# A two-block network in float32 on one core: another order of the first loads

## The chip, the cores and the metric

The kernel runs on one core of one Trainium2 chip. The metric is the device time of one execution, in microseconds (us).

## The reference, cut to what matters

Two blocks run one behind the other on 256 tokens of 1024 features. The first has two layers; a context of 256 tokens goes through the first of them too, so that layer works on 512 columns. What the change touches is how a layer of the first block begins:

```python
mod = (silu_c @ w_mod[layer] + b_mod[layer])[:, None, :]
shift1, scale1, gate1, shift2, scale2, gate2 = jnp.split(mod, N_MOD, axis=-1)
h = modulate(rms_norm(x, norm_mix[layer]), shift1, scale1)   # h * (1 + scale) + shift
q, k, v, hy, g = jnp.split(h @ w_in[layer], PROJ_SPLITS, axis=-1)
...
h = jnp.sin(freq[0] * (z @ fw1 + fb1))                        # the hyena filter
h = jnp.sin(freq[1] * (h @ fw2 + fb2))
h = jnp.sin(freq[2] * (h @ fw3 + fb3))
h = (h @ fw4).reshape(length, 2, HYENA_WIDTH)
h = h * decay[:, None, :]
```

The filter does not depend on x. Its spectrum (a discrete Fourier transform) is wanted for the long convolution in the middle of the layer. Behind attention, convolution, gates and a feed-forward network of two layers comes a second block, which ends in a mixture of 32 experts whose weights alone are some 200 MB.

## The kernel before, in words

The data lie feature-major: 128 features on the partitions, tokens along the free axis. A weight tile (`u`, 128x1024 float32, 512 KB) holds 128 columns of a weight for all 1024 rows. Most products take float32 in two parts: ACT rounds a tile to its upper part (`u<-u`, fp32r), DVE subtracts it to get the lower part, and TensorE does three matmuls (upper by upper, upper by lower, lower by upper). Modulation tiles (`w_mod`) and the filter's are used as plain float32; such a matmul leaves two records in the trace.

Nothing is scheduled by hand. Generators (`modulation`, `statistics`, `spectra`, `hy_vx` and others) yield what their next step reads. `drive` steps the first of them whose inputs are there by a built-in estimate of each engine's time (`Timer`), and the engines then do their instructions in the order in which they were written. `Stream` loads weight tiles ahead of their use, `loads` of them, on SyncE's queue. All DMA issues of SyncE stand in one queue, and each new one also waits until the one eight issues of the queue before it has landed, since eight semaphores go round. All operations are written by one helper, line 288, so nearly every row of the trace reads L288 and instructions are known by their tiles.

At the start of `program`, SyncE issues the filter's three small inputs (`z`, `filt_w1`, `filt_w23`; `load_filter`), the column parameters (`cols`), the identity (`ident`) and x in four tiles (`load_x`). Then `layer` steps `spectra` once, which issues the filter's last weight w4 and its decay, and drives three generators together:

- `modulation(0, 0)`: 16 tiles of `w_mod`, two matmuls each (`ps<-u,cs`; two tiles use different column groups of TensorE), then a copy by ACT, four transposes, and DVE makes `mod` and `gmix`, the gain columns. `loads` is set by hand in it: eight modulation tiles ahead in the first half, a DFT table after the second step, three weight tiles from the fourth.
- `statistics`: ACT squares x (eight times `t<-u` or `acc<-u`, 128x512), DVE adds them up in `acc`, TensorE sums over the partitions with a column of ones, DVE and GpSimd take the reciprocal root, TensorE spreads it (`ps<-ident,s`), DVE multiplies x by it.
- `spectra`: three rounds of matmul (`ps<-t`, 128x256), reduction of the angle by DVE, and a sine by ACT (`t<-t`, 128x256); then the matmuls with w4 (`ps<-u,t`) and the two layers' spectra (`ps<-u`).

When the first two are through, `modulated` makes the layer's input: for each pair of chunks ACT scales half of it (`t<-t,mod,gmix`), DVE the other half, ACT takes the upper part (`u<-t`) and DVE the lower. `hy_vx` then starts the first projection with two weight units side by side (48 matmuls), and what is left of `spectra` runs beside it.

Of the kernel before, what the change touches and what calls it, by code (L numbers as in the profile page):

```python
# [19 lines left out]
KC = D // 128  # L20
# [13 lines left out]
# ---------------------------------------------------------------- host layout  # L34
# [6 lines left out]
def _units(w):  # L41
    """[K, N] -> [N/128, 128 rows, K/128, 128 columns]"""
    k, n = w.shape
    return np.ascontiguousarray(w.reshape(k // 128, 128, n // 128, 128).transpose(2, 1, 0, 3))


def column_parameters(p):
    """Every per-feature vector as columns of one [128, n] array, and where each one starts."""
# [32 lines left out]
def shape_tables():  # L81
    t = {}
    # axial rotary embedding of the first block, feature-major; the sign of the pair swap is in the sine
# [8 lines left out]
    # discrete Fourier transform on odd frequencies  # L92
# [7 lines left out]
    # filter positions and decay  # L100
# [10 lines left out]
    # rotary embedding of the second block: inverse frequency and sign of the swapped half, per partition  # L111
# [4 lines left out]
    # 8 * log of how many of the dilated branches let query i see key j  # L116
# [6 lines left out]
    # before[t', t] = t' < t; descending weights that break ties; slot numbers  # L123
# [45 lines left out]
# ---------------------------------------------------------------- order of the program  # L169

class Null:
    """Stands for every object of the program in the pass that only finds the order of the weight tiles."""
# [22 lines left out]
class Part:  # L195
    """The two float32r parts of a tile.  ready: the n pieces of the program that fill it are there; eta: when they
    are expected to have run."""
# [15 lines left out]
class Timer:  # L213
    """Estimates when each engine will be through with its instructions, and when each tile will be there."""
# [60 lines left out]
class Engine:  # L275
    """An engine whose instructions are also given to the timer."""
# [26 lines left out]
class Stream:  # L303
    """The weight tiles that one chain of generators uses, in their order.  Loads run ahead; a unit (128 columns) is
    split ahead into two float32r parts."""
# [20 lines left out]
    def prepare(self):  # L326
        """split the next unit"""
# [8 lines left out]
    def run(self):  # L336
        """loads and splits ahead"""
# [13 lines left out]
    def get(self, *key, unit=True):  # L351
        """the next tile: a generator, which ends with the tile, or with the two parts of a unit"""
# [23 lines left out]
class Squares:  # L376
    """Sums of the squares of x for each token.  x comes in four pairs of chunks, each [128, 2, T] cut as gemm cuts
    its output; the first three are added up before they are summed over the partitions"""
# [39 lines left out]
class Net:  # L418
# [28 lines left out]
    # ---- allocation  # L447
# [16 lines left out]
    def ahead_of(self, n):  # L464
        """split n weight units ahead"""
        self.W.loads, self.W.splits = n + self.MORE, n

    # ---- order of the instructions
    def defer(self, fn, *deps, engine="DVE"):
        """fn emits instructions of an engine once deps are expected to be there when the engine comes to them"""  # L470
        self.pending.append((deps, engine, fn))

    def tick(self):
        """deferred instructions whose inputs are there; loads and splits of weights"""
# [22 lines left out]
    def force(self):  # L497
        """the deferred instructions whose inputs are there first"""
        e = min(self.pending, key=self.when)
        self.pending.remove(e)  # L500
        e[2]()
# [9 lines left out]
    def stall(self, deps):  # L511
        """how long the tensor engine would wait"""
# [3 lines left out]
    def step(entry):  # L516
        """one step of [generator, what the step reads]; False if it can do nothing yet, None at its end"""
# [7 lines left out]
    def drive(self, *gens, extra=()):  # L525
        """all of the generators to their ends: the first of those whose inputs are there makes a step.  A generator
        yields what its next step reads, or BLOCK.  extra: entries that come second, but need not end"""
# [25 lines left out]
    def fill(self, *queues):  # L553
        """a step of the first entry of a queue, if its inputs are there"""
# [11 lines left out]
    def background(self):  # L566
        """a step of the work that only has to be done some time later"""
# [3 lines left out]
    def wait(self, *deps):  # L571
        """steps of the fillers while the tensor engine would wait"""
# [5 lines left out]
    def run(self, gen):  # L578
        """a generator to its end, with the fillers in its gaps"""
# [13 lines left out]
    # ---- pieces  # L593
    def divide(self, items, parts=(), then=None):
        """hi = float32r(src), lo = src - hi for each (hi, lo, src) or (hi, lo, src, factor of src); then the
        parts are ready"""
# [26 lines left out]
    def gemm(self, keys, xs, T=512, n=None, cuts=None, together=False, stream=None):  # L623
        """unit . xs for each weight unit, as a list of PSUM tiles [128 features, n units, T]; a generator.  xs may
        still grow to n; with cuts xs is a list of lists, and the k range between two cuts has its own output;
        together: the units side by side, each chunk of xs used as soon as it is there"""
# [50 lines left out]
    def pair(name, *idx, tail=()):  # L677
        """the two units of a pair of chunks: the last index counts pairs"""
# [3 lines left out]
    def by_tile(t, T):  # L682
        """[128, 2 chunks, T] cut as gemm cuts its output"""
# [5 lines left out]
    def pairs(self, T):  # L689
        """an endless row of tiles [128, 2, T]"""  # L690
# [5 lines left out]
    def chunks(self, n, T, pieces=1):  # L696
        """n places for the two float32r parts of [128, T]; and the parts of each two as gemm cuts its output"""
# [1663 lines left out]
```

## Time and profile before

| | |
|---|---|
| median of 3 runs | 2087.15 us (2084.54 to 2092.17) |
| span of the profiled execution | 2082.8 us; its own time is not listed apart |
| TensorE busy | 1986.3 us, 95% of the span |
| TensorE busy in the first 51 us | 36.57 us |
| DMA rate from 1700 to 1800 us | 419 GB/s |

A timeline row tells the start of a group of like instructions, the time from the group's start to its end, the engine, the operation with its tiles and sizes, how many there are, and, in brackets, how long the engine stood idle before it and what ended that. A window row tells busy times of the engines, the granted clock of TensorE (1.00 is full speed), the share of the DMA engines and their rate. A busy TensorE is not one at its peak, since ends of matmuls are modelled.

### The profile page before, as it was taken

What the parts mean: (1) busy time and instruction counts of PE and PEld (TensorE: products, weight loads), DVE (VectorE), ACT (ScalarE), POOL (GpSimd) and SP (SyncE); (2) the same over time, 40 slices, a digit from 0 to 9 for tenths busy, and PEclk for the clock granted to TensorE, in tenths of its full rate; (3) what the DMA queues carried; (4) which work ended last, traced back from release to release, by engine and by line L of the source; (5) the groups of instructions that cost most, each with busy time, mean ns of one, the idle gap of its engine ahead of it and who ended that gap; (6) DMA issues with size and microseconds to landing.
All of it is one profiled execution on the core that took longest, in us unless ns stands there. A gap on an engine that the chain in (4) does not pass through costs nothing. (4 is left out here: it accounts for less than half of the span.)

```text
span 2082.8 us, 28349 instructions
## 1 busy us (share of the span) xinstructions
PE 1986.3 (95%) x11415; PEld 1450.8 (70%) x11415; DVE 945.7 (45%) x1624; ACT 718.3 (34%) x1171; POOL 39.8 (2%) x49
## 2 busy tenths in 40 slices
PE   7999999999999999999999999999999898888886
PEld 3777877776778888889888999998799541111111
DVE  6665755145334333576764755568654310000001
ACT  3433665224222322363653543444734110000001
POOL 0000000000000000000000000000010000000000
PEclk9999999999999999999999999999999999999999
DMA  9423224464223233444357455553257999999997
GB/s 366 132 81 101 62 82 150 164 236 174 96 88 114 89 91 100 134 170 149 114 188 245 164 189 172 178 183 94 100 167 295 377 419 420 419 419 419 419 420 318
DMA packets 121438, 432.13 MB, mean 207 GB/s; under 512 B 13654, under 2 KB 14152, under 8 KB 121304
## 3 DMA queue, kind: packets, MB, share of 16 engines
q1 hardware_dynamic: 119464, 424.64, 55.7%
q0 software_dynamic: 1696, 5.38, 0.8%
q8 instruction: 91, 1.49, 0.3%
q14 instruction: 43, 0.35, 0.0%
q10 hardware_dynamic: 144, 0.26, 0.0%
HBM read 428.13 MB, written 2.10 MB: 207 GB/s over the span
## 5 line engine op out<-in xcount | busy, mean ns | idle before, releaser
L288 PE MATMUL ps<-u 128*128 128x256 f32 (+2 forms) x9088 | 1599.8, 345 | 28.1 <-DMA u<-w 15.9
L288 PEld LDWEIGHTS ps<-u 128*128 128x128 f32 (+1 forms) x9088 | 1289.0, 186 | 348.1 <-DMA u<-w 101.3
L288 DVE TENSOR_TENSOR u<-u 128x1024 fp32r<-128x1024 f32 (+4 forms) x414 | 433.1, 1071 | 269.6 <-ACT u L288 226.2
L288 ACT ACTIVATE u<-u 128x1024 fp32r<-128x1024 f32 (+3 forms) x392 | 360.3, 960 | 286.9 <-DVE u L288 237.0
L288 PE MATMUL ps<-u,t 128*32 128x512 f32 (+1 forms) x1028 | 214.9, 610 | 30.8 <-DMA u<-w 18.2
L288 PEld LDWEIGHTS ps<-u,t 128*32 128x32 f32 (+1 forms) x1028 | 44.2, 110 | 185.8 <-DMA u<-w 114.5
L288 ACT ACTIVATE u<-ps 128x512 f32<-128x512 f32 (+3 forms) x207 | 91.7, 488 | 237.0 <-PE ps L288 236.3
L288 DVE TENSOR_TENSOR t<-t,ps 128x512 f32<-128x512 f32 x12 | 8.3, 688 | 258.9 <-PE ps L288 258.9
L288 ACT ACTIVATE t<-ps 128x512 f32<-128x512 f32 x57 | 33.4, 595 | 252.5 <-PE ps L288 252.4
L288 DVE TENSOR_TENSOR u<-u,ps 128x512 f32<-128x512 f32 x53 | 36.4, 687 | 128.4 <-PE ps L288 128.3
L288 PE MATMUL ps<-u,cs 128*32 128x512 f32 x384 | 86.1, 644 | 0.0
L288 DVE TENSOR_TENSOR u<-ps,u 128x128 fp32r<-128x128 f32 (+2 forms) x135 | 59.6, 491 | 48.9 <-ACT u L288 42.7
L288 DVE SCALAR_TENSOR_TENSOR u<-ps,mod,u 128x256 f32<-128x256 f32 x96 | 41.7, 479 | 79.9 <-PE ps L288 79.6
L288 ACT ACTIVATE u<-t 128x512 fp32r<-128x512 f32 (+1 forms) x74 | 41.8, 592 | 102.9 <-DVE t L288 91.7
L288 ACT ACTIVATE u<-ps,s 128x512 fp32r<-128x512 f32 (+1 forms) x26 | 15.8, 640 | 149.0 <-PE ps L288 145.8
L288 DVE SCALAR_TENSOR_TENSOR u<-ps,s,u 128x512 fp32r<-128x512 f32 (+2 forms) x24 | 15.4, 662 | 113.2 <-ACT u L288 90.9
L288 ACT ACTIVATE t<-ps,s 128x256 f32<-128x256 f32 (+1 forms) x80 | 49.1, 620 | 41.2 <-DVE s L288 40.2
L288 POOL TENSOR_TENSOR s<-s,mhalf 128x4 f32<-128x4 f32 (+2 forms) x25 | 28.5, 1141 | 1608.4 <-DVE s L288 1527.1
L288 PE MATMUL ps<-ident,t 128*128 128x128 f32 x332 | 46.8, 275 | 9.5 <-DVE t L288 7.0
L288 ACT ACTIVATE t<-u 128x512 f32<-128x512 f32 x41 | 25.2, 627 | 85.3 <-DVE u L288 85.2
L288 PEld LDWEIGHTS ps<-ident,t 128*128 128x128 f32 x332 | 37.8, 141 | 23.6 <-DVE t L288 14.3
L288 DVE TENSOR_REDUCE s<-ps 128x1 f32<-128x512 f32 (+2 forms) x65 | 38.9, 621 | 33.2 <-PE ps L288 32.9
(126 smaller groups left out, 682.6 us busy)
## 6 DMA issues: line engine op xcount, KB each, us to landing
u<-w SPq DMA_DIRECT2D x381, 512.0 KB, 9.9
u<-w_in SPq DMA_DIRECT2D x102, 512.0 KB, 3.9
u<-w_mod SPq DMA_DIRECT2D x96, 512.0 KB, 5.0
u<-w_gu SPq DMA_DIRECT2D x88, 512.0 KB, 3.7
u<-w_dn SPq DMA_DIRECT2D x32, 512.0 KB, 3.5
u<-w_out SPq DMA_DIRECT2D x24, 512.0 KB, 4.5
u<-w_oa SPq DMA_DIRECT2D x16, 512.0 KB, 4.0
u<-w_dn SPq DMA_DIRECT2D x16, 384.0 KB, 3.1
```

Of the source, the lines that this page charges most:

```text
L288: return fn(*args, **kw)
```

## The change

SyncE's queue takes the column parameters, four modulation tiles, x, the other twelve modulation tiles, and only then weight tiles, the DFT table, w4 and the decay. The filter's small inputs and the identity go out on ACT's queue. w4 and the decay are allocated and issued behind the third sine. The settings of `loads` that mixed the streams by hand are gone. All comments and docstrings are blanked. Cut to its core:

```diff
@@ modulation
             if (l, grp) == (0, 0):
-                self.W_dft.loads = min(k // 2, 1)
-                self.W.loads = 0 if k < 4 else 3
-                self.W_mod.loads = 8 if k < 4 else 2 * (KC - k)
+                self.W_mod.loads = 2 * (KC - k)
@@ load_filter
         for t, name in ((z, "z"), (w1, "filt_w1"), (w23, "filt_w23")):
-            self.nc.sync.dma_start(t, self.a[name])
+            self.nc.scalar.dma_start(t, self.a[name])
@@ spectra
         nc, a = self.nc, self.a
-        w4, dec = self.u([128, 1024]), self.u([128, 2, 512])
-        for t, name in ((w4, "filt_w4"), (dec, "decay")):
-            nc.sync.dma_start(t, a[name])
         h = z
         for i, w in enumerate((w1, w23[:, :128], w23[:, 128:])):
             yield (w, h)
             ps = self.ps()[:, :256]
             nc.tensor.matmul(ps, w, h, start=True, stop=True)
             h = self.sin_of(ps, i)
+        w4, dec = self.u([128, 1024]), self.u([128, 2, 512])
+        for t, name in ((w4, "filt_w4"), (dec, "decay")):
+            nc.sync.dma_start(t, a[name])
@@ layer
             self.step(start[0])
-            self.W.loads = self.W_dft.loads = 0
             self.drive(self.modulation(0, 0), statistics(), extra=start)
@@ program
-            filt = self.load_filter()
             self.cols = cp.tile([128, a["cols"].shape[1]], F32, name="cols")
             nc.sync.dma_start(self.cols, a["cols"])
+            filt = self.load_filter()
             self.ident = cp.tile([128, 128], F32, name="ident")
-            nc.sync.dma_start(self.ident, a["ident"])
-            self.load_x()
+            nc.scalar.dma_start(self.ident, a["ident"])
+            for n in (4, 16):
+                self.W_mod.loads = n
+                self.W_mod.run()
+                if n == 4:
+                    self.load_x()
```

The order that the generators fall into changes with it. On ACT, at the start of the program, `t<-t` are the sines, `acc<-u` and `t<-u` the squares of x, `t<-ps` the copy of the modulation. Before:

```order
L288 ACTIVATE identr<-ident 128x128
L288 ACTIVATE t<-t 128x256
L288 ACTIVATE acc<-u 128x512
L288 ACTIVATE t<-u 128x512 x3
L288 ACTIVATE t<-t 128x256
L288 ACTIVATE t<-u 128x512 x4
L288 ACTIVATE t<-t 128x256
```

and now, with the four loads ahead:

```order
L288 DMA t<-z 33x256
L288 DMA t<-filt_w 33x128
L288 DMA t<-filt_w 128x256
L288 DMA ident<-ident 128x128
L288 ACT_TABLE_LOAD
L288 ACTIVATE cs<-cols 128x8 x2
L288 ACTIVATE identr<-ident 128x128
L288 ACTIVATE t<-t 128x256 x3
L288 ACTIVATE acc<-u 128x512
L288 ACTIVATE t<-u 128x512 x7
L288 ACTIVATE t<-ps 128x512
```

All three sines now stand ahead of the first square.

On TensorE from the start, `ps<-t` are the filter's matmuls, `ps<-ones` the sums of squares, `ps<-u,cs` the modulation, `ps<-ident,s` the spread, `ps<-u,t` those with w4, `ps<-u` spectra and projection. Before:

```order
L288 MATMUL ps<-t 128x256 x2
L288 MATMUL ps<-ones,t 128x1 x8
L288 MATMUL ps<-ones,acc 128x1 x4
L288 MATMUL ps<-t 128x256
L288 MATMUL ps<-u,cs 32x512 x2
L288 MATMUL ps<-ident,s 128x128 x4
L288 MATMUL ps<-u,cs 32x512 x16
L288 MATMUL ps<-u,t 128x512 x2
L288 MATMUL ps<-u,cs 32x512 x2
```

and now:

```order
L288 MATMUL ps<-u,cs 32x512 x4
L288 MATMUL ps<-t 128x256
L288 MATMUL ps<-ones,t 128x1 x4
L288 MATMUL ps<-ones,acc 128x1 x4
L288 MATMUL ps<-ones,t 128x1 x4
L288 MATMUL ps<-u,cs 32x512 x6
L288 MATMUL ps<-ident,s 128x128 x4
L288 MATMUL ps<-u,cs 32x512 x18
L288 MATMUL ps<-ident,t 128x128 x4
L288 MATMUL ps<-u,t 128x512 x4
L288 MATMUL ps<-u 128x512 x72
```

The whole modulation and half of the matmuls with w4 now stand ahead of the first `ps<-u`. (The first rows of now: one `ps<-t`, four `ps<-u,cs`, one `ps<-t`, and then those shown.)

On ACT at the end of `modulated`, `u<-u` of 128x1024 is the upper part of a weight tile or table. Before, one of them stands directly ahead of the chain over the four pairs:

```order
L288 ACTIVATE t<-ps 128x512
L288 ACTIVATE u<-ps 128x512
L288 ACTIVATE u<-u 128x1024
L288 DMA rope_t<-rope 128x512
L288 ACTIVATE t<-t,mod_95,gmix_374 128x256 x2
L288 ACTIVATE u<-t 128x512 x2
```

and now behind its last pair:

```order
L288 ACTIVATE t<-t,mod_127,gmix_303 128x256 x2
L288 ACTIVATE u<-t 128x512 x2
L288 ACTIVATE u<-u 128x1024 x3
L288 ACTIVATE u<-u 128x512 x2
L288 ACTIVATE u<-u 128x1024 x2
```

The three are the DFT table and the second and third weight tiles; the first weight tile's upper part still stands ahead of the chain, where before those of the first two and of the table did.

## Rows read from the trace of the kernel before

**Rows 1.** The page, part 1: busy us (share) and instructions.
```profile
PE 1986.3 (95%) x11415; PEld 1450.8 (70%) x11415; DVE 945.7 (45%) x1624; ACT 718.3 (34%) x1171; POOL 39.8 (2%) x49
```
**Rows 2.** Windows: stretch, length, busy times of engines, clock, DMA share, GB/s.
```profile
0.00:51.00 51.00, 36.57 (x146) 17.04 (x146) 34.36 (x75) 19.67 (x36) 1.22 (x5) 1.00 0.95 373
51.00:200.00 149.00, 149.00 (x701) 116.57 (x700) 89.18 (x141) 55.84 (x86) 3.66 (x3) 1.00 0.30 100
...
1700.00:1800.00 100.00, 89.55 (x386) 21.49 (x385) 6.34 (x11) 5.72 (x10) 0.58 (x1) 1.00 1.03 419
```
**Rows 3.** Waits of SyncE's queue, 1560 to 1700 us: total, times, longest.
```profile
SPq L288 <- PE ps L288: 45.1, 32, 7.6
```
**Rows 4.** Waits of TensorE, 51 to 450 us.
```profile
PE ps L288 <- ACT t L288: 1.7, 3, 0.9
```
**Rows 5.** Timeline of TensorE, 0 to 64 us.
```profile
15.29 3.57 PE L288 MATMUL ps<-ones,t 128*128 128x1 f32 x16 [5.51 <-ACT t L288]
...
20.43 1.20 PE L288 MATMUL ps<-t 128*128 128x256 f32 x2
21.56 1.92 PE L288 MATMUL ps<-u,cs 128*32 128x512 f32 x4
23.41 1.12 PE L288 MATMUL ps<-ident,s 128*128 128x128 f32 x4
24.46 4.64 PE L288 MATMUL ps<-u,cs 128*32 128x512 f32 x32
...
41.25 1.05 PE L288 MATMUL ps<-u,cs 128*32 128x512 f32 x4
...
46.45 3.70 PE L288 MATMUL ps<-u,t 64*128 64x512 f32 x8
...
51.06 11.18 PE L288 MATMUL ps<-u 128*128 128x512 f32 x48
```
**Rows 6.** Timeline of SyncE's queue, 0 to 46 us.
```profile
0.75 0.43 SPq L288 DMA_DIRECT2D t<-z  x1
...
2.93 1.85 SPq L288 DMA_DIRECT2D u<-xT  x4
...
17.91 9.08 SPq L288 DMA_DIRECT2D u<-w_mod  x8
```
**Rows 7.** Timeline of ACT, 0 to 58 us.
```profile
9.23 0.63 ACT L288 ACTIVATE acc<-u 128x512 f32<-128x512 f32 x1 [0.73 <-DMA u<-xT]
9.77 1.85 ACT L288 ACTIVATE t<-u 128x512 f32<-128x512 f32 x3
13.26 0.42 ACT L288 ACTIVATE t<-t 128x256 f32<-128x256 f32 x1 [1.64 <-issue]
...
26.67 1.06 ACT L288 ACTIVATE u<-u 128x1024 fp32r<-128x1024 f32 x1 [1.13 <-DMA u<-dft]
...
43.84 0.59 ACT L288 ACTIVATE t<-ps 128x512 f32<-128x512 f32 x1
...
45.23 1.05 ACT L288 ACTIVATE u<-u 128x1024 fp32r<-128x1024 f32 x1
46.17 1.08 ACT L288 ACTIVATE t<-t,mod,gmix 128x256 f32<-128x256 f32 x2
...
53.23 1.14 ACT L288 ACTIVATE u<-t 128x512 fp32r<-128x512 f32 x2
```
**Rows 8.** Timeline of DVE, 0 to 58 us.
```profile
9.81 0.54 DVE L288 TENSOR_SCALAR t<-ps,cols 128x256 f32<-128x256 f32 x1 [1.76 <-PE ps L288]
...
12.88 0.29 DVE L288 TENSOR_SCALAR t<-t 128x256 f32<-128x256 f32 x1
...
45.38 0.25 DVE L288 SCALAR_TENSOR_TENSOR gmix<-mod,cols 128x8 f32<-128x8 f32 x2
...
48.17 1.22 DVE L288 TENSOR_TENSOR u<-u 128x1024 fp32r<-128x1024 f32 x1
```
**Rows 9.** A window around a fall of the granted clock, columns as in rows 2.
```profile
210.00:216.00 6.00, 6.00 (x40) 6.00 (x39) 4.52 (x13) 1.45 (x3) 1.64 (x1) 0.72 0.29 90
```

## The prediction

> **What bounds the kernel now.** I read the busy times first: TensorE is busy 95% of the span [rows 1]. The windows then show where it is not. In the first 51 us it works 36.57 us; from 51 to 200 us it works without a gap; near the end the DMA engines run at 419 GB/s, their share at 1.03 [rows 2]. So there are two limits: TensorE from 51 us on, and the experts' weights at the end. Before that end SyncE's queue waits mostly for TensorE (45.1 us between 1560 and 1700 us) [rows 3], so that stream starts when TensorE comes to it. A microsecond lost or won at the start is therefore a microsecond at the end, as long as nothing between takes it up; TensorE's waits between 51 and 450 us are 1.7 us in all [rows 4]. At most 51 - 36.57 = 14.4 us could be won, and only in the first 51 us. The timelines of TensorE, ACT, DVE and SyncE's queue for that stretch [rows 5 to 8] give the sum.
>
> **What the change moves.** Matmuls, and all other work, stay the same in number; two small scalings go from ACT to DVE. The order of all engines differs up to the first layer's output projection and is the same behind it. What differs is the path to the first projection of the layer, 48 matmuls at 51.06 us [rows 5], and what has been done by then.
>
> **Step 1, when the tiles land.** Before, the first 512 KB tile is issued at 2.93 us, behind five small loads [rows 6], and ACT, waiting for it, starts at 9.23 us. Eight modulation tiles are issued in 9.08 us, the last taking 0.33, so one per 1.25 us: each issue waits for an older tile. Tile n should land at 9.2 + 1.25 x (n - 1); for the first DFT table (n = 15) that is 26.7 us, and ACT, waiting for it, starts at 26.67 [rows 7]. Now the first big tile follows one small issue of 0.43 us and goes at 1.2 us. The gain lies between nothing (the small loads still move) and 2.93 - 1.2 = 1.73 us; I take 1.1, because 0.25 MB of small loads at 420 GB/s is 0.6 us. So the second modulation tile lands at 9.35 us, the last of the 16 (n = 20) at 31.9, the first two weight tiles at 33.1 and 34.4, the filter's w4 (n = 27) at 40.6.
>
> The Trainium skill (DMA: Bandwidth & Descriptors, Issuing engines are not separate DMA queues) says that loads issued by several engines run on the same 16 DMA engines, and that issuing from more of them saves only issue time. By it the other queue brings no bandwidth, and with the whole 1.73 us saved the result would be 0.6 us lower; the trace of before, with one queue at the start, cannot show it.
>
> **Step 2, the sines stand ahead of the squares.** This decides the forecast. Before, ACT does one sine, squares half of x, and so on. Now the three sines come first and the eight squares of x behind them; on TensorE the filter's second matmul stands behind two modulation tiles, and four modulation tiles stand ahead of the third. Its engines work in their order, so: second tile 9.35, plus the 1.85 us from the first modulation tile's start to the next kind of work (21.56 to 23.41) [rows 5], is 11.2; the matmul 1.20 gives 12.4; DVE's reduction of the angle takes 12.88 + 0.29 - 9.81 = 3.36 [rows 8], to 15.8; the sine 0.42 [rows 7], to 16.3; once more 1.20, 3.36, 0.42 and small gaps, 21.4. The squares take 1.85 / 3 = 0.62 each [rows 7], the seventh ends at 25.7, and TensorE's sums of squares start. They take 20.43 - 15.29 = 5.1 [rows 5]: 30.9. Behind them stand three modulation tiles (in two goes, 3.7 at the 1.85 above; 1.7 at 4.64 / 8 = 0.58), the spread of the norm (23.41 to 24.46, 1.05), and nine more tiles (9 x 0.58 = 5.2) [rows 5]. With 3.7 the modulation ends at M = 30.9 + 3.7 + 1.05 + 5.2 = 40.8 us. All its tiles landed by 31.9: the DMA, for which the change makes room, is not what ends last. Before, M is 41.25 + 1.05 = 42.3 [rows 5].
>
> **Step 3, from M to the projection.** ACT's copy starts at 43.84 and the gain columns are ready at 45.38 + 0.25 [rows 7, 8]: 1.8 us. ACT's chain of x's upper parts runs from 46.17 to 53.23 + 1.14: 8.2 us [rows 7]. Before, the split of the second weight tile (45.23) ran ahead of that chain. Now the DFT table's and the second weight tile's stand behind it, 1.05 each: M + 12.1. DVE's lower part of it comes behind the table's, 1.22 each [rows 8]: M + 13.5 = 54.3 us. The first projection takes both weight tiles side by side, so until then TensorE can do five of its matmuls and four with w4, and waits.
>
> **Step 4, what is owed by then.** Before, by 51.06 us TensorE had also done four fp32 matmuls with w4 (3.70, two records each), the 24 of the first spectrum (at 11.18 / 48 = 0.233: 5.6) and one tile of the next modulation (1.05); now it has five of the projection's (1.2) ahead [rows 5]. Owed: 3.7 + 5.6 + 1.05 - 1.2 = 9.15. The shift is 54.3 + 9.15 - 51.06 = +12.4 us.
>
> **Step 5, the clock.** Between about M + 5 and M + 13.5 TensorE now has almost nothing. At 210 to 216 us, behind a short wait and single-column sums, the granted clock reads 0.72 on average [rows 9]: between 2.4 and 1.2 GHz that is 6 x 0.28 x 2 = 3.4 us at the lower level. Such a stretch on full work costs half, 1.7; two cost 3.4; none costs nothing. I take 2.0, since the spectrum's splits would hold TensorE up a little anyway. Sum: **+14.4 us**.
>
> The Trainium skill (TensorE: Matmul & The Clock Gate, HAM oscillation) says that a TensorE that waits for its data comes back at the lower clock, each time. By it the stretch behind the wait starts at 1.2 GHz and the sum is +14.4; were the clock kept, it would be +12.4.
>
> **Small edits.** The four issues on ACT's sequencer end before the column parameters land, for which ACT waits anyway, and the first sine is not what step 2 waits for: nothing. If that cover were gone, each would cost its 0.43 us [rows 6]. w4 lands at 40.6 us, before TensorE comes to it (M + 0.6 + 0.7), and the wait of step 3 would cover several microseconds more. Blanked comments cost nothing.
>
> **To the time.** The span becomes 2082.8 + 14.4 = 2097.2. The profiled execution's own time is not listed; the median of the three runs (2084.5 to 2092.2) lies 2087.15 - 2082.8 = 4.35 above its span, which I keep: **2101.5 us**.
>
> **Rivals.** (a) *The short chain*, which ends as no change. If the first tiles land so early that no matmul of the filter waits for them, the sines run on from the second, which before ended at 13.26 + 0.42 [rows 7]: 13.7 + 5.0 = 18.7. Then the seventh square ends at 23.0, the sums at 28.1, and with the three tiles at 1.7 M = 28.1 + 1.7 + 1.05 + 5.2 = 36.1. If the clock holds too, the shift is 36.1 + 13.5 + 9.15 - 51.06 = +7.7, 2095 us. For it: the slow prices of step 2 are from a stretch in which TensorE had just begun. Against: it wants lower bounds in three places at once. It decides for "no change" from M under 38.8 with the clock kept, 36.8 without. (b) *DVE becomes the bound.* Of DVE's 34.36 us before 51 us [rows 2], the filter's products and the spectrum's splits now fall behind 54 us, together with the weight splits. If TensorE then waits for splits by 6 us (an estimate: five of its splits of a weight tile, at 1.22 [rows 8]), it is +20, 2108. Against it: DVE was busy only 89.18 of 149 us from 51 to 200 [rows 2]. (c) *A gain.* Were the modulation done when its tiles are there, at 33, and all else hidden, w4 at 40.6 would still stand first on TensorE: 40.6 + 3.7 + 9.15 + 1.2 - 51.06 is +3.6. The start can't give 10 us; only waits of the later order could, and before there are 1.7 us of them [rows 4].
>
> **How the numbers follow.** Forecast (M 38 to 42; 2096 to 2106): 0.60. Short chain (2089 to 2097): 0.25. DVE bound (2104 to 2113): 0.13. A gain: 0.02. The bounds of step 1 move M by -0.6 to +1.1, the three tiles by -2.0, the clock the sum by -2.0 to +1.4. The range 2091 to 2109 leaves out the gain and the ends of (a) and (b). About 0.5%, 10.4 us, is what a measurement of this kernel can tell from no change. Slower by more (over 2097.6): 0.52 of the forecast's 0.60 and all of (b), together 0.65. Within: the rest and (a), 0.33. Faster: 0.02.
>
> **What would show it.** In the profile after: squares of x on ACT from about 21 us, behind the third sine; sums on TensorE from about 26; the last of the 16 modulation tiles' matmuls at 40 or so, though landed near 32; a gap of 5 us or more on TensorE between 46 and 54, ended by ACT or DVE with the second weight tile; a clock under 1.00 behind it. Wrong would be: squares at 13 us, M near 33, or no gap before the projection. If all that holds and the time is unchanged, the start is not passed on to the end.

## The result, and the profile after

The changed kernel takes 2104.78 us (median of 4 runs, 2099.77 to 2104.99), the kernel before beside it 2088.4 us (4 runs): a ratio of 1.0063, with a 95% interval of 1.0048 to 1.0079, so slower by 16.4 us. 2101.5 us was forecast, in a range of 2091 to 2109.

The page of the profiled execution of after (span 2103.0 us, own time 2104.8), busy us (share) and instructions, against [rows 1]:

```profile
PE 1997.7 (95%) x11415; PEld 1456.5 (69%) x11415; DVE 946.4 (45%) x1626; ACT 716.8 (34%) x1169; POOL 39.8 (2%) x49
```

As many matmuls as before, and 11.4 us more busy time in them. Of these, 6.3 us arise by the point near 80 us at which TensorE has done the same matmuls in both (72.58 us busy for 66.26): part of the loss is matmuls at the lower clock. The windows, columns as in [rows 2] (length, busy times of TensorE, its weight loads, DVE, ACT, GpSimd, then granted clock, DMA share, GB/s):

```profile
0.00:51.00 51.00, 30.91 (x115) 12.92 (x115) 29.31 (x67) 19.60 (x36) 1.22 (x5) 0.76 0.89 354
...
45.00:50.00 5.00, 3.85 (x6) 1.16 (x4) 4.45 (x8) 5.00 (x9) 0.00 (x0) 0.50 0.35 143
50.00:55.00 5.00, 4.48 (x10) 3.09 (x11) 4.80 (x7) 1.19 (x2) 0.00 (x0) 0.50 0.00 0
```

In the first 51 us TensorE works 30.91 us where it was 36.57 before [rows 2], and the clock, 1.00 before, reads 0.76. The reading of 1.00 at the very start is doubtful: 16 of the single-column sums take 3.57 us at 15.29 us before [rows 5], as long as at the lower clock here (8 in 1.87). From 45 to 55 us the clock is at 0.50, the lower of the two levels, all the time. TensorE's timeline, against [rows 5]:

```profile
24.51 1.87 PE L288 MATMUL ps<-ones,t 128*128 128x1 f32 x8 [7.54 <-ACT t L288]
...
33.20 0.65 PE L288 MATMUL ps<-ident,s 128*128 128x128 f32 x4
33.78 4.49 PE L288 MATMUL ps<-u,cs 128*32 128x512 f32 x36
...
41.66 5.61 PE L288 MATMUL ps<-u,t 64*128 64x512 f32 x8 [2.04 <-DMA u<-filt_w]
47.20 1.65 PE L288 MATMUL ps<-u 128*128 128x512 f32 x3
50.29 1.22 PE L288 MATMUL ps<-u 128*128 128x512 f32 x2 [1.44 <-ACT u L288]
51.74 17.93 PE L288 MATMUL ps<-u 128*128 128x512 f32 x67 [0.23 <-DVE u L288]
```

The sums of squares wait 7.54 us for ACT and start 9.2 us later than before. The 16 modulation tiles end at M = 33.78 + 4.49 = 38.27. Then TensorE does only four transposes, four matmuls with w4 and five of the projection in 13.5 us, and its long run starts when the second weight tile's parts are there. The timeline of ACT shows both causes, against [rows 7]:

```profile
10.05 0.31 ACT L288 ACTIVATE identr<-ident 128x128 fp32r<-128x128 f32 x1 [5.00 <-DMA ident<-ident]
...
20.41 0.42 ACT L288 ACTIVATE t<-t 128x256 f32<-128x256 f32 x1 [4.61 <-DVE t L288]
20.73 0.61 ACT L288 ACTIVATE acc<-u 128x512 f32<-128x512 f32 x1
21.25 3.73 ACT L288 ACTIVATE t<-u 128x512 f32<-128x512 f32 x7
38.31 0.60 ACT L288 ACTIVATE t<-ps 128x512 f32<-128x512 f32 x1 [13.33 <-PE ps L288]
...
48.25 2.93 ACT L288 ACTIVATE u<-u 128x1024 fp32r<-128x1024 f32 x3
```

The squares stand behind the third sine, and the table and the second and third weight tiles behind the chain over x. The first row is new: ACT waits 5.00 us for the identity, a load of 64 KB that it issued itself.

**How the runs below are read.** The last part of the program adds differences that do not follow the start. One row near its beginning is the same in all kernels; before and after:

```profile
1479.33 1.05 PE L288 MATMUL ps<-ones,t 128*128 128x1 f32 x8 [0.18 <-ACT t L288]
```

```profile
1494.31 1.05 PE L288 MATMUL ps<-ones,t 128*128 128x1 f32 x8 [0.18 <-ACT t L288]
```

From that row to the end of the span it takes 603.5 us in the profile of before and 608.7 in that of after, and between 603.5 and 612.1 in the fourteen profiles of this study, in no order that follows the start. So each kernel is told by three numbers: the shift near 80 us (when TensorE has done equally many matmuls and modulation tiles as before; after: +12.2), the shift of the row above (after: +15.0), and the difference of the medians (after: +16.4). The first two come from one profile of each kernel. The medians are each taken against runs of the kernel before from the same round; most ratios overlap, so that differences of 1 or 2 us between two kernels rest on the profiles alone.

| kernel | near 80 us | at 1479 us | medians | ratio (95%) |
|---|---|---|---|---|
| after | +12.2 | +15.0 | +16.4 | 1.0063 (1.0048 to 1.0079) |
| e1, squares first | +11.9 | +12.8 | +15.5 | 1.0069 (1.0047 to 1.0091) |
| e2, split first | +10.2 | +11.3 | +12.3 | 1.0058 (1.0041 to 1.0074) |
| e12, both | +9.8 | +12.0 | +10.4 | 1.0052 (1.0032 to 1.0072) |
| e4, small loads on SyncE | +11.4 | +14.2 | +13.7 | 1.0062 (1.0044 to 1.0079) |
| e5, before, small loads on ACT | +3.2 | +3.0 | +6.5 | 1.0034 (1.0021 to 1.0047) |
| e6, filter's loads early | +6.5 | +5.4 | +6.5 | 1.0034 (1.0019 to 1.0048) |
| e10, e6 and small loads on SyncE | +7.6 | +9.1 | +6.3 | 1.0029 (1.0018 to 1.0041) |
| e11, extra matmuls | +11.4 | +12.2 | +12.9 | 1.0068 (1.0052 to 1.0083) |
| e13, e6 and squares between sines | +15.0 | +20.1 | +18.8 | 1.0086 (1.0067 to 1.0105) |
| e14, e13 and small loads on SyncE | +15.1 | +20.1 | +19.6 | 1.0086 (1.0067 to 1.0104) |
| e16, e14 and split first | +4.3 | +4.4 | +2.8 | 1.0014 (1.0005 to 1.0023) |
| e15, before, squares first | -1.1 | -1.9 | -2.0 | 0.9996 (0.9984 to 1.0009) |

### The profile page after: what moved, and what is told of

Its sections match the earlier page's. It is cut to its first block, busy times and chain, and to the rows that moved or that the text cites. A ratio compares the mean times of both kernels' runs of the same rounds, so it can differ in the third digit from the quotient of the medians.

```text
span 2103.0 us, 28358 instructions
## 1 busy us (share of the span) xinstructions
PE 1997.7 (95%) x11415; PEld 1456.5 (69%) x11415; DVE 946.4 (45%) x1626; ACT 716.8 (34%) x1169; POOL 39.8 (2%) x49
```

## The experiments

The theory of the forecast: the three sines ahead of the squares hold up the modulation (step 2), the second weight tile's split behind ACT's chain holds up the projection (step 3), and the filter's work is owed behind it (step 4). The rivals: the landing of tiles, DVE as the bound, and the small loads' queue.

**e1: the squares ahead of the sines again**

```diff
@@ layer
+            for p in range(KC // 2):
+                self.squares(sums, T)(p)
             self.step(start[0])
@@ statistics
-                for p in range(KC // 2):
-                    yield (self.xp[p],)
-                    self.squares(sums, T)(p)
+                yield (self.xp[3],)
```

> The changed kernel with one edit: ACT's eight squares of x stand ahead of the three sines again, SyncE's order of loads is kept. If the sines ahead of the squares delay the modulation (step 2), the squares start when x lands (12 to 15 us), the sums of squares end by about 23, and the modulation ends about 1.5 us behind its last tile (landed near 31.4): M near 33 in place of 38.3. Step 3 (M + 13.5) is untouched, so the long run of matmuls starts near 47 and the shift against the kernel before at the 80 us mark falls from +12.2 to about +7, a time near 2100 (after: 2104.8). If the landing of tiles or the filter's own matmuls hold the modulation instead, M stays at 37 to 39 and the time at 2103 to 2106.

The modulation ended earlier, at 35.0 us, but nothing came of it. TensorE's and then ACT's timeline:

```profile
18.41 1.87 PE L288 MATMUL ps<-ones,acc 128*128 128x1 f32 x8 [4.47 <-DVE acc L288]
...
31.36 3.64 PE L288 MATMUL ps<-u,cs 128*32 128x512 f32 x32
```

```profile
38.39 0.42 ACT L288 ACTIVATE t<-t 128x256 f32<-128x256 f32 x1 [7.71 <-DVE t L288]
...
38.71 0.58 ACT L288 ACTIVATE t<-ps 128x512 f32<-128x512 f32 x1
```

The sums start 6.1 us earlier and M is 3.3 us earlier. But the copy of the modulation (38.71; 38.31 in after) now stands behind the third sine, and this behind a reduction that DVE makes last of all. One order of ACT was exchanged for another that holds the same copy. The time, 2105.11 us, is that of the second expectation, though M is not. So this run doesn't tell what step 2 costs.

**e2: the second weight tile split ahead of the chain**

```diff
@@ layer, behind the modulation
             nc.scalar.dma_start(self.rope_t, self.a["rope"])
+            while not self.dry and self.W.split < 2:
+                self.W.prepare()
```

> The changed kernel with one edit: the second weight tile's split stands ahead of ACT's chain over x again (step 3). M stays at 38.3. If that split is what TensorE waits for, the first projection starts near M + 8.7 (before: 51.06 against 42.3), paced by DVE's lower parts until about M + 14, the gap of TensorE between 47 and 51.7 us shrinks to under 2 us, and the time falls by 5 to 9 us, to 2096 to 2100. If DVE is the bound (it has eight lower parts of x and two of weights to make at about M + 13), the projection only runs in pieces, the gap is spread over several waits and the time falls by under 3 us.

Nearer to the second expectation: 2.0 us won near 80 us, 3.7 at 1479 us, 2.8 to 4.1 in the medians (2101.94 for 2104.78, or against before in each round). TensorE's timeline, then DVE's:

```profile
41.83 0.50 PE L288 MATMUL ps<-u 128*128 128x512 f32 x1 [2.73 <-ACT u L288]
45.15 9.15 PE L288 MATMUL ps<-u 128*128 128x512 f32 x29 [2.82 <-DVE u L288]
```

```profile
42.13 2.36 DVE L288 TENSOR_TENSOR u<-u 128x1024 fp32r<-128x1024 f32 x2
44.40 4.90 DVE L288 TENSOR_TENSOR u<-t,u 128x512 fp32r<-128x512 f32 x8
```

The projection starts 6.6 us earlier, but its second matmul waits until 45.15 us for x's first lower part, which stands behind two lower parts of weights on DVE. Behind that wait the clock reads 0.50 from 45 to 50 us, so that 29 matmuls take 9.15 us (6.7 at the rate of before), and the w4 matmuls, which filled the gap of after, now stand behind. The gap was not empty enough for the whole of it to come back.

**e12: both**

> Both edits at once: squares ahead of sines, and the second weight tile's split ahead of the chain. If steps 2 and 3 make up the loss and add, M is near 33, the projection starts near 42, the shift at 80 us is 0 to +4 and the time 2088 to 2093, about the kernel before (2088.4). If the small loads on ACT's queue or the landing of the tiles were the cause, at least half of the loss stays: 2097 or more.

2100.01 us, 10.4 over before, is in the range of the second expectation. That doesn't show the two causes that it names, for which e4 and e6 below are the test. M is 34.0, the chain starts at 40.12 us as in e2 (40.18), held by the third sine as in e1. The two edits don't add.

**e4: the small loads back on SyncE's queue**

```diff
@@ load_filter, program
-            self.nc.scalar.dma_start(t, self.a[name])
+            self.nc.sync.dma_start(t, self.a[name])
-            nc.scalar.dma_start(self.ident, a["ident"])
+            nc.sync.dma_start(self.ident, a["ident"])
```

> The changed kernel with one edit: the filter's three small inputs and the identity go out on SyncE's queue behind the column parameters, ahead of the first modulation tile; the order of instructions on TensorE, ACT, DVE and GpSimd is exactly that of the changed kernel. If the late landing of the small loads on ACT's queue (identity 7.9 us from issue to landing, SyncE's next big loads held behind it) costs something, the identity lands by about 5 us, the sines start 2 us earlier, and since squares, sums and modulation stand behind the sines, M falls by 1 to 2 us and so does the time: 2103 to 2104. By step 1 alone (first tile 1.7 us later) M would rise by up to 1.7 and the time be 2105 to 2107.

As the first expected, if a little less: 0.8 us won near 80 us, M 37.6. The order on all four compute engines is that of after. In the changed kernel the queue of the small loads is worth about 1 us there.

**e5: the kernel before, with the small loads on ACT's queue** (the same edit the other way round, in the kernel before)

> The kernel before with one edit: the filter's three small inputs and the identity go out on ACT's queue; SyncE begins with the column parameters and x. The order of instructions on TensorE, ACT, DVE and GpSimd is exactly that of the kernel before. If the other queue is harmless or helps, x is issued 1.7 us earlier and the time is 2087 to 2090 (before 2089.6 in the last comparison). If small loads on ACT's queue land late whenever SyncE has big ones in flight, the identity lands at 8 us or later in place of 4 to 5, the first sine slips by 3 to 5 us, and the modulation, whose tiles land until 41 us anyway, takes up most of it: a shift of 0 to +3 us at the 80 us mark.

The order on all four compute engines is that of before, so this is the price of the queue alone, with the sharing of semaphores that comes with it (last section): +3.2 us near 80 us, 1.0034 (1.0021 to 1.0047). DMA issues of the first 12 us (KB each, median us from issue to landing), before and then e5:

```profile
ident<-ident SPq DMA_DIRECT2D x1, 64.0 KB, 2.2
```

```profile
ident<-ident ACTq DMA_DIRECT2D x1, 64.0 KB, 6.9
```

TensorE's timeline of e5, against [rows 5]:

```profile
5.22 1.19 PE L288 MATMUL ps<-t 33*128 33x256 f32 x2 [5.22 <-DMA t<-filt_w]
...
17.05 3.58 PE L288 MATMUL ps<-ones,t 128*128 128x1 f32 x16 [5.51 <-ACT t L288]
...
39.08 2.50 PE L288 MATMUL ps<-u 128*128 128x512 f32 x5 [2.56 <-DVE u L288]
```

The small loads land among the big ones; the first sine, and so the sums, come 1.8 us later (17.05 for 15.29). At 39 us a wait has become 2.56 us long, and the five matmuls behind it take 2.50 where before they took 1.44.

**e6: w4, decay and the DFT table behind x again, as before**

```diff
@@ program
                 if n == 4:
                     self.load_x()
+                    self.w4dec = self.u([128, 1024]), self.u([128, 2, 512])
+                    for t, name in zip(self.w4dec, ("filt_w4", "decay")):
+                        nc.sync.dma_start(t, a[name])
+                    self.W_dft.run()
@@ spectra
-        w4, dec = self.u([128, 1024]), self.u([128, 2, 512])
-        for t, name in ((w4, "filt_w4"), (dec, "decay")):
-            nc.sync.dma_start(t, a[name])
+        w4, dec = self.w4dec
```

> The changed kernel with one edit: w4, the decay and the first DFT table are issued behind x and ahead of the other twelve modulation tiles (as before), in place of behind the weight tiles. The three sines still stand ahead of the squares and the small loads stay on ACT's queue. The filter's matmuls with w4 and half of the first spectrum then stand between the modulation tiles again, and the second weight tile's split ahead of ACT's chain. If the loss is that this work was moved behind the modulation (it is owed, and TensorE has nothing to do while x's parts are made), M rises to 40 to 43 but the first projection starts at 49 to 52 with nothing owed, the gap is gone, the clock holds, and the time is 2086 to 2092, as before. If sines ahead of squares or the small loads' queue were the cause, it stays at 2096 or more.

This takes away 9.9 of the 16.4 us in the medians (6.5 are left), and 5.7 of the 12.2 near 80 us. 2095.25 lies between the two expectations, just under the second. TensorE's timeline:

```profile
23.65 1.87 PE L288 MATMUL ps<-ones,t 128*128 128x1 f32 x8 [7.54 <-ACT t L288]
...
47.73 1.05 PE L288 MATMUL ps<-u,cs 128*32 128x512 f32 x4
...
57.54 11.18 PE L288 MATMUL ps<-u 128*128 128x512 f32 x48
```

The sums still wait 7.54 us for ACT. M is 48.8, 6.5 us later than before, and the projection 8.8 us behind it, with nothing owed and with no long gap, at a clock of 1.00 from 35 us on. So with M ten us later than in after the kernel is ten us faster: it matters more what is done by M than when M is. After the first 9 us TensorE never waits for a modulation tile here, so their landing, which the change improves, doesn't hold it. M came later than expected, and the 6.5 us that stay are what the start of the change still costs.

**e10: e6 with the small loads on SyncE's queue** (the edit of e4)

> The last one, and the small loads on SyncE's queue behind the column parameters: what is left of the change is four modulation tiles ahead of x and the sines ahead of the squares. If both causes hold, 0.5 to 1.5 us less than with the filter's loads early alone, 2085 to 2091. If the small loads don't matter, the same within 0.5 us.

No gain, as the second expected: the medians are the same (2095.03 and 2095.25). Near 80 us it is 1.1 us worse. TensorE waits 2.30 us for the first modulation tile, until 7.62 us (6.03 in e6), and the filter's second matmul stands behind that tile and the next.

**e11: the clock**

```diff
@@ layer, behind the modulation
+            idle = self.ps()
+            for i in range(5):
+                nc.tensor.engine.matmul(idle, self.ident, self.xp[0][:, 0], start=True, stop=True)
             nc.scalar.dma_start(self.rope_t, self.a["rope"])
```

> The changed kernel, and behind the modulation's four transposes five extra float32 matmuls of x with the identity (128x512, into a tile that nobody reads; 0.93 us each by the matmuls with w4), which fill TensorE's wait for w4 (2.0 us) and part of that for the second weight tile. No other instruction moves. If the clock costs the long run of matmuls 2.0 to 2.5 us (17.93 us for 67 matmuls against 16.62 x 67/72 = 15.5), it keeps 1.00, the run takes 15.5 to 16 us and the shift at 80 us is +9.5 to +10.5. If the clock falls all the same, the extra matmuls delay those with w4 and the time is the same or up to 4 us longer.

Here the kernel does five matmuls more than the computation needs. TensorE's timeline:

```profile
39.72 4.46 PE L1400 MATMUL ps<-u,ident 128*128 128x512 f32 x10
44.11 3.70 PE L288 MATMUL ps<-u,t 64*128 64x512 f32 x8
...
50.57 0.73 PE L288 MATMUL ps<-u 128*128 128x512 f32 x2 [1.87 <-ACT u L288]
52.01 16.82 PE L288 MATMUL ps<-u 128*128 128x512 f32 x67 [0.72 <-DVE u L288]
```

The extra matmuls fill the 2.04 us of waiting for w4 and push the w4 matmuls 2.45 us back, but these now take 3.70 us in place of 5.61 and end only 0.5 us later. The run of 67 takes 16.82 in place of 17.93. It doesn't reach 15.5: the clock reads 1.00 from 39 to 50 us, but behind the two waits that are left it fell once more (0.66 from 50 to 55 us). So nearly half of the clock's price in that run could be bought back, 0.8 us at 80 us since the run starts 0.3 later. Both expectations are missed by size, the first is right in kind.

**e13 and e14: what is left without the filter's late loads and the sines ahead of the squares**

```diff
@@ layer (e13, beside e6; statistics as in e1)
             self.step(start[0])
+            for p in range(KC // 2):
+                if p % 2 == 0:
+                    self.step(start[0])
+                self.squares(sums, T)(p)
```

> The changed kernel with two edits: w4, the decay and the first DFT table issued right behind x (the edit that alone gave a shift of +6.5 us at the 80 us mark), and the squares of x between the sines as before (one sine, four squares, one sine, four squares, the third sine). What is left of the change is the small loads on ACT's queue and four modulation tiles ahead of x. If the sines ahead of the squares make those 6.5 us (the sums start at 23.7 where before they start at 15.3), the sums start near 18 and the shift falls to +2.5 to +4, 2090 to 2093. If the small loads' queue makes them, it stays at +5.5 to +6.5, 2094 to 2096.

> The last one, and the small loads on SyncE's queue behind the column parameters; the order on TensorE, DVE and GpSimd is the same. What is left of the change is four modulation tiles ahead of x. If the small loads on ACT's queue cost what they cost in the kernel before (+3.2 us at 80 us, where that was the only edit), the shift falls by another 2 to 3 us, to between 0 and +1. If they only cost where x comes first, the two are the same within 1 us.

Both expectations of e13 failed, and the first of e14: these are the slowest kernels of all. That the two are the same within 1 us, the second of e14, holds. The sums do start at 17.67 and 16.50 us, yet M is 48.1 and 47.9, near e6's, and then TensorE, here of e14, stands still:

```profile
46.84 1.06 PE L288 MATMUL ps<-u,cs 128*32 128x512 f32 x8
...
56.07 1.06 PE L288 MATMUL ps<-u,cs 128*32 128x512 f32 x8
62.60 0.80 PE L288 MATMUL ps<-u 128*128 128x512 f32 x1 [5.47 <-ACT u L288]
65.67 23.71 PE L288 MATMUL ps<-u 128*128 128x512 f32 x95 [2.27 <-DVE u L288]
```

The planner, which goes by its own estimates, had again put the second weight tile's split behind the chain, and this time also behind the parts of the second layer's filter, which DVE makes until 65 us: ACT splits that tile at 64.98 us, 17 us behind M (49.20 us in after, 11 us behind M). And the 6 us by which the sums start earlier than in e6 were gone before M. On TensorE's timeline of e13,

```profile
23.83 1.86 PE L288 MATMUL ps<-ones,acc 128*128 128x1 f32 x8 [3.02 <-DVE acc L288]
...
29.01 3.78 PE L288 MATMUL ps<-u,t 64*128 64x512 f32 x4
```

3.0 went into a wait for DVE's adds, which now stand behind the third reduction, and the w4 matmuls, two groups of 3.78 us at a clock of 0.50 (29 to 38 us), had taken 1.98 each in e6. As in e1 another wait hides what the earlier squares are worth; e16 below shows it. The two kernels are equal within 0.1 us at both marks, so in these orders the small loads' queue costs nothing.

**e15: the kernel before, with the second sine behind all eight squares**

```diff
@@ program
+            nc.sync.dma_start(self.cols, a["cols"])
             filt = self.load_filter()
-            nc.sync.dma_start(self.cols, a["cols"])
@@ layer (statistics as in e1)
             self.step(start[0])
+            self.step(start[0])
+            for p in range(KC // 2):
+                self.squares(sums, T)(p)
+            self.step(start[0])
```

> The kernel before with two small edits: the column parameters ahead of the filter's inputs on SyncE's queue, and ACT's second sine behind all eight squares (before: behind four). Nothing else moves on any engine. Before, TensorE works without a gap of more than 1.2 us from the sums of squares at 15.29 us on, and these wait for ACT. If that start is what sets the first stage, the sums start at 13.5 to 14.5 us and the shift at 80 us is -0.8 to -1.6, a time 1 us below before, which the median can hardly show. If landing tiles set it, the shift is 0.

```profile
12.71 3.57 PE L288 MATMUL ps<-ones,t 128*128 128x1 f32 x16 [2.42 <-ACT t L288]
17.61 1.87 PE L288 MATMUL ps<-ones,acc 128*128 128x1 f32 x8 [1.33 <-DVE acc L288]
...
78.65 1.05 PE L288 MATMUL ps<-u,cs 128*32 128x512 f32 x4
```

Near 80 us TensorE's timeline moves as expected, by 1.1 us (79.70 before). At the sums it moves by 2.6 us, more than expected, of which 1.3 are lost to DVE's adds. The order on TensorE, DVE and GpSimd is that of before. So sums that start earlier do bring something where nothing else is in the way. The median is 2.0 us lower, but with 0.9984 to 1.0009 the times alone don't show it. It is the lowest median of all kernels here.

**e16: e14, with the second weight tile's split ahead of the chain** (the edit of e2)

> The kernel of the last run but one (filter's loads behind x, squares between the sines, small loads on SyncE's queue) with one more edit: both first weight tiles are split ahead of ACT's chain over x. There the modulation ended at 47.9 us, but the order again put the second weight tile's split behind the chain, and TensorE had 8.6 us without work (57.1 to 65.7, but for one matmul) before its run of 95. If that split is what it waited for, the first projection starts near M + 9, at 56 to 58 us, the gap is under 2 us and the time falls by 7 to 13 us, to 2096 to 2101. If DVE's lower parts are the bound there, as in the changed kernel with the same edit (2 to 3 us won), the gap moves behind the first matmuls and the time stays at 2104 to 2107.

```profile
46.07 1.07 PE L288 MATMUL ps<-u,cs 128*32 128x512 f32 x8
...
55.32 11.21 PE L288 MATMUL ps<-u 128*128 128x512 f32 x48
```

The first expectation, and more: 15.5 us less than e14 (2093.13 for 2108.64), 10.8 of it near 80 us. There is no gap left, and the projection starts at M + 8.2. The edit puts one split of ACT and its counterpart on DVE ahead, and the planner then orders what follows differently too, so at most the part near 80 us can be put to the split alone. Here the same edit brings about five times what it brought in e2 near 80 us. In e14 the split stood behind the second layer's filter too. And unlike in e2, the spectrum and the w4 matmuls keep TensorE busy until 55.32 us, while DVE makes the weight's lower parts, and the clock reads 1.00 from 50 us on.

e16 also gives the price of step 2. Against e10 the order of the engines differs only at the start: the squares stand between the sines in place of behind them, and the second split is ahead of the chain in both. TensorE's timeline of e10, then of e16:

```profile
24.81 1.86 PE L288 MATMUL ps<-ones,t 128*128 128x1 f32 x8 [7.54 <-ACT t L288]
...
48.87 1.05 PE L288 MATMUL ps<-u,cs 128*32 128x512 f32 x4
```

```profile
16.88 3.41 PE L288 MATMUL ps<-ones,t 128*128 128x1 f32 x16 [1.01 <-ACT t L288]
23.04 1.87 PE L288 MATMUL ps<-ones,acc 128*128 128x1 f32 x8 [2.75 <-DVE acc L288]
```

The sums start 7.9 us earlier, M falls from 49.9 to 47.1, and the shift from +7.6 to +4.3 near 80 us and from +9.1 to +4.4 at 1479 us. So sines ahead of the squares cost about 3.3 us here. What is left in e16 are four modulation tiles ahead of x and, against before, DVE's adds of the squares behind the third reduction, at 1.0014 (1.0005 to 1.0023).

## Why the prediction was right

**Step 1, landing.** The first modulation tile went out at 1.19 us (1.2 forecast), the last of the 16 had landed near 31 (31.9), w4 at 41.66 (40.6). That the modulation tiles' landing is not what ends last is what e6 shows most plainly. The landing of w4 does hold TensorE, for 2.04 us, which the longer wait behind it covers, as forecast.

**Step 2, sines ahead of squares.** The sequence was as told, most terms somewhat too large: the squares took 0.53 each for 0.62, the spread 0.58 for 1.05, the nine tiles 4.49 for 5.2. M is 38.27 for 40.8. But "this decides the forecast" was too strong: e10 and e16 put the sines ahead of the squares at 3.3 of the 12.2 us near 80 us. In e1 and e13 the squares were moved too and nothing was won, since what stands behind them (the third sine ahead of the copy, DVE's adds, a lower clock, a later split) took it up.

**Step 3, from M to the projection.** M + 13.5 was forecast; it is 51.74 - 38.27 = 13.47. e2 shows that the split is waited for, but that in the changed kernel DVE stood right behind it, which is rival (b) in small; e16 against e14 shows what the split can cost when nothing stands behind it.

**Step 4, work owed.** 38.27 + 13.47 + 9.15 - 51.06 is +9.8; with the 2.5 of step 5 it is +12.3, where +12.2 was measured. What each part of the change costs is told by taking them off one after the other: after, small loads back (e4), filter's loads and table early (e10), squares between the sines (e16). The shift near 80 us goes 12.2, 11.4, 7.6, 4.3, and at 1479 us 15.0, 14.2, 9.1, 4.4. So the late filter loads, with the debt and the late split that they bring, are the largest part of what was taken off (3.8 and 5.1 us), step 2 comes next (3.3 and 4.7), and neither decides alone. In another order of the edits the shares would be others, as e13 shows.

**Step 5, the clock.** 2.0 forecast; the run of 67 took 17.93 us, where at the rate of before (16.62 us for 72) it is 15.47: 2.5. The clock reads 0.50 until 55 us and 0.81 from 55 to 60. The Trainium skill (TensorE: Matmul & The Clock Gate, HAM oscillation) says of a matmul kernel that waits for data in each of its steps that every step starts at the lower clock. e11, which fills one wait and brings the run from 17.93 to 16.82 us, agrees.

**What the sum left out.** +12.2 near 80 us, where +14.4 was forecast, and then +15.0 at 1479 us: 2.8 us are lost later. The prediction had no waits behind 80 us; there is one of 3.01 us where the longest before was 0.9 [rows 4], with the sums behind it at the lower clock (0.61 from 216 to 222 us), as in [rows 9]. TensorE's timeline of after:

```profile
217.44 3.57 PE L288 MATMUL ps<-ones,t 128*128 128x1 f32 x16 [3.01 <-ACT t L288]
```

Where half of the first spectrum is done ahead of the projection and no long gap is left, as before (e5, e6, e10, e15, e16), the shift at 1479 us is within 1.5 us of that near 80; in the other seven it is 0.8 to 5.1 above it. So the forecast had M 2.5 us too late and missed the later wait, and the two nearly cancel: +14.4 forecast, +15.0 at 1479 us. That they do is luck. The time is 3.3 us above the forecast: 1.25 of it because before's own median was 2088.4 here and 2087.15 there, the rest because the medians differ by 16.4 where 14.4 was forecast.

**Small edits.** "Nothing" for the small loads on ACT's queue was argued from the issue, 0.43 us each, and not from the landing. In the changed kernel it is 0.8 us (e4); as an edit alone it is 3.2 us and 0.34% (e5). The step that failed is the cover: ACT's wait for the column parameters, until 3.4 us, hides the issues, but behind it ACT waits for the identity until 10.05.

**Rival (a)** needed M under 36.8 without the clock; M was 38.27 and the clock was lost. **Rival (b)** has the measured time in its range too (2104 to 2113); the profile decides against it, as TensorE waits only 0.23 us for DVE ahead of its long run, where (b) needs 6. **Rival (c)** is excluded by the result.

What stays open: how the 4.3 us that are left in e16 divide, and how much of the 1 to 5 us behind 80 us belongs to each later wait. The trace of e16 shows three things that before doesn't have: x's first tile is squared at 12.39 us (9.23 before), behind the four modulation tiles; TensorE waits 2.75 us for DVE's adds; and from 28 to 38 us the clock reads 0.50, so that two groups of w4 matmuls take 3.78 us each (1.98 before). No run takes one of them away alone.

## What to carry to other kernels

When loads are put in another order, ask first which engine work they feed and what that work was hiding: here w4 and a table, loaded early, filled the time in which the first projection's operands were made, and loaded late they left a gap and a debt. The place of one split in an in-order queue was worth 11 us near 80 us in one order and 2 in another, so look at what stands ahead of the first consumer, and at the second engine right behind it, before counting a gain. A step that comes earlier is worth only what the next steps of its chain let through: eight squares moved ahead brought nothing in two orders and 3.3 us in a third. So don't give up a cause because one edit against it failed; look at what took the gain, and take that off too.

## What the runs showed of the hardware that was not expected

Small loads on a second queue land late when the first queue has big ones in flight: the identity, 64 KB, took 2.2 us from issue to landing on SyncE's queue and 6.9 (e5) and 7.9 (after) on ACT's, though issued at about the same time (2.46 and 2.12 us). And SyncE's queue is held by them too. Its waits in the first 60 us of after (total, times, longest), none of which is in the waits of before:

```profile
SPq L288 <- DMA t<-filt_w: 3.3, 2, 2.3
...
SPq L288 <- DMA ident<-ident: 1.2, 1, 1.2
```

SyncE's timeline of after, against [rows 6], shows what that does:

```profile
1.19 2.13 SPq L288 DMA_DIRECT2D u<-w_mod  x4
3.39 5.49 SPq L288 DMA_DIRECT2D u<-xT  x4
10.05 11.67 SPq L288 DMA_DIRECT2D u<-w_mod  x12
```

The four tiles of x take 5.49 us to issue (1.85 before), and the next modulation tile goes out at 10.05 us, when the identity has landed. The semaphores in the trace's records tell why: eight go round, and here the loads of both queues take them in turn. The fifth modulation tile's issue waits for semaphore 105, which the identity's load had, the second and fourth x tiles' for those of the filter's inputs (102, 104). So it is the program's sharing of semaphores that makes SyncE's queue wait for ACT's loads; why those land so late, the trace doesn't say.
